# Scanning a state space mixer by rotated states: one scan instruction per block of eight chunks

## The chip, the cores and the metric

The kernel runs on one core of a Trainium2 chip. The metric is device time in microseconds (us) of one execution, given as the median of several runs. The engines are named as the profile names them: PE (TensorE matmul), PEld (its weight loads), DVE (VectorE), ACT (ScalarE), POOL (GpSimd) and SP (SyncE, which issues the DMAs).

## The reference

One inference step of a two-layer decoder trunk over 1,024 prompt tokens and 8 x 4 sample tokens, with a width of 1,024. The change is in one part of layer 0, the state space mixer (S5): 32 groups of 16 channels, each of which drives 64 complex states with a diagonal transition.

```
bu = einsum(u, b_bar)                        # per token: 64 complex inputs per group
s_t = a_bar * s_(t-1) + bu_t                 # complex, elementwise
y_t = Re(c s_t) + D u_t;   out = gelu(y) * sigmoid(gelu(y) @ W + b)
```

Beside it layer 0 has a retention (4 heads) that reads the same normalised input; both outputs go through one projection. Then follow a gated convolutional MLP, layer 1 (a gated linear recurrence with 8 heads) and a second MLP.

## The kernel before, in words

The dense products are made of fp32 numbers split in two parts, three matmuls for each tile of 128 x 128 weights and up to 384 tokens. A job is one weight tile: three token chunks of 24 matmuls each. A planner written by hand puts all other work between these matmuls: a clock `now` counts one unit for a chunk of 24 matmuls, and `at(dt, fn)` emits `fn` when this clock has gone on by `dt`. In layer 0 the order is fixed by these times alone; in layer 1 the planner also looks at its own estimate of what is ready. Each engine runs its instructions in the order in which they were emitted.

The S5 part cuts the 1,024 tokens into 128 chunks of 8. The 32 groups lie along the free dimension, the real parts of the 64 states on partitions 0 to 63 and the imaginary parts on 64 to 127. Its stages:

- `s5_setup` (before the first tile ends) works out the transition and its powers 0 to 8 (`ar`, `ai`) in tiles of 128 x 32; `s5_b` the input matrices; `s5_setup2` the powers 1 to 8 of the transition over one chunk (`mr`, `ms`).
- `s5_x`, 16 pairs of groups: POOL builds a matrix (`va`, `vb`), PE transposes it, ACT copies it (`vt`), PE multiplies it with the chunk's inputs into a PSUM tile `px`. ACT writes the 128 chunk states to `sall`, DVE the sample columns to `xs`. Four calls of `u_work` issue four pairs each.
- `s5_within`, 4 x 7 steps: the 128 chunks are taken as 16 blocks of 8, and step j adds the transition times position j-1 to position j, in all 16 blocks of 8 groups at once. Each step is a complex multiply and add (`s5_mac`: five DVE instructions on 128 columns, two of them on half of the partitions).
- `s5_samples`, one such step for the sample tokens. `s5_carry`, 15 steps in series: the last position of a block gets the last position of the block before, times the transition over a block (five DVE instructions on 32 columns).
- `s5_y`, 16 pairs in 8 calls: `s5_spread` adds the block's incoming state to its other 7 positions (five DVE instructions on 210 columns), POOL, PE and ACT build the output matrices (`ca`, `tz`), and `prod` multiplies `ca` with `sall` and `tz` with the inputs on PE; DVE adds the skip term into `ysh`, and SP stores it.

While these run, PE works on the last tile of the input projection and on those of q, k and v of the retention; DVE and ACT empty their PSUM tiles (`acc`, four buffers, and `misc`, four buffers), and POOL makes part of the weights' low halves (`wlo`) and of the rotary products (`qr`).

Of the kernel before, what the change touches and what calls it, by code (L numbers as in the profile page):

```python
# [10 lines left out]
F32 = mybir.dt.float32  # L11
F32R = mybir.dt.float32r
I32 = mybir.dt.int32
U8 = mybir.dt.uint8
AF = mybir.ActivationFunctionType
OP = mybir.AluOpType
# [30 lines left out]
     "f0": 0.1, "x00": 0.604, "x01": 0.303, "x02": 0.446, "x03": 0.3, "e1": -0.169, "e2": -0.006, "w0": 0.325, "w": 0.274, "sm": 0.432, "ca": 0.308, "ys": 0.020, "r0": 1.195, "rs": 5.046, "h0": 0.1, "hs": 6.5,  # L47
# [183 lines left out]
class Trunk:  # L231
# [414 lines left out]
    def layer0(self):  # L646
# [124 lines left out]
        def u_work(rt):  # L771
            t = P[f"x0{rt}"] + P["x"] * 2 * rt - 3.0 * max(rt - 1, 0)
            x1, x2 = P["x1"] + P["e1"] * (rt == 0), P["x2"] + P["e2"] * (rt == 0)
            for i in range(2):
                self.s5_x(2 * rt + i, t + P["x"] * i, 0.5 * P["x"], x1, x2)
            t += 1.5 * P["x"] + x1 + x2 + P["w0"]
            for j in range(1, 8):
                self.at(t + P["w"] * j, lambda j=j: self.s5_within(8 * rt, 8, j), None,
                        lambda: "powers" not in self.held and self.xdone >= 4 * (rt + 1), "within")
            if rt < 3:  # L780
                return
            t += 7 * P["w"] + P["sm"]
            self.at(t, self.s5_samples, None, lambda: self.xdone == 16)
            for b in range(1, 16):
                self.at(t + P["ca"] * b, lambda b=b: self.s5_carry(b), None,
                        lambda: list(self.wdone.values()) == [7] * 4, "carry")
            for u in range(8):
                self.s5_y(u, t + 15 * P["ca"] + P["ys"] + P["y"] * u, 0.5 * P["y"])
# [137 lines left out]
    def s5_alloc(self):  # L926
        nc, sp = self.nc, self.s5
        self.sall = sp.tile([128, SG, 137], F32, name="sall")
        self.xs = sp.tile([128, SG, NB], F32, name="s_xs")
        nc.gpsimd.memset(self.sall[:, :, 8:9], 0.0)  # L930
# [24 lines left out]
    def s5_load(self):  # L955
        self.nc.sync.dma_start(self.xs, self.I["st_s5"])
        self.bin = []
        for g, n in ((0, 12), (12, 12), (24, 8)):
            t = self.tmp("bin")[:, :2 * n * SH]
            self.nc.sync.dma_start(t.rearrange("p (a c) -> p a c", a=2), self.I["b_in"][:, :, SH * g:SH * (g + n)])  # L960
            self.bin.append(t.rearrange("p (a g h) -> p a g h", a=2, h=SH))
        self.at(0.1, lambda: self.nc.gpsimd.tensor_copy(self.sall[:, :, 0:8], self.xs))

    def s5_setup2(self):

        nc = self.nc
# [27 lines left out]
    def s5_setup(self):  # L994
        nc, sp = self.nc, self.s5
        n = SG

        def small(s):
            return sp.tile([128, n], F32, name=s, tag=s)
        dt, mag, ang, sn, cs = (small(s) for s in ("s_dt", "s_mag", "s_ang", "s_sn", "s_cs"))  # L1000
        lre, lim = self.v("lre"), self.v("lim")
        t = self.tmp("set")
        t = [t[:, n * i:n * i + n] for i in range(9)]
        et, ct = t[:4] + [t[4].bitcast(I32)], t[5:]
# [12 lines left out]
        self.mr = sp.tile([128, SG, 8], F32, name="mr")  # L1017
        self.ms = sp.tile([128, SG, 8], F32, name="ms")
        self.mixed(lambda: self.powers(ar, ai, 1), self.s5_inputs)

    def s5_inputs(self):
# [48 lines left out]
    def s5_x(self, u, t, dt, x1, x2):  # L1070
# [28 lines left out]
        def prod(p, vt):  # L1099
# [9 lines left out]
            nc.scalar.activation(self.sall[:, G, 9:137], pv[:, :, 0:128], AF.Copy)  # L1109
            nc.vector.tensor_copy(self.xs[:, G, :], pv[:, :, 128:136])  # L1110
# [15 lines left out]
    def s5_blocks(self, g, n):  # L1126

        return self.sall[:, g:g + n, 9:137].rearrange("p g (b j) -> p g b j", j=8)

    def s5_samples(self):  # L1130
# [3 lines left out]
        self.s5_mac(self.nc.vector, self.xs, self.sall[:, :, 0:8], self.ar[:, :, 4:5], self.si4[:, :, None], sh, t)  # L1134
        self.put(self.O["s5s"], self.xs)

    def s5_within(self, g, n, j):
        assert "powers" not in self.held and self.xdone >= (g + n) // 2 and self.wdone.get(g, 0) == j - 1
        self.wdone[g] = j
        x = self.s5_blocks(g, n)  # L1140
        sh = [128, n, 16]
        t = [self.tmp("s_t")[:, :16 * n].rearrange("p (g b) -> p g b", b=16) for i in range(2)]
        G = slice(g, g + n)
        self.s5_mac(self.nc.vector, x[:, :, :, j], x[:, :, :, j - 1], self.mr[:, G, 0:1], self.ms[:, G, 0:1], sh, t,
                    self.nc.gpsimd if P["wi"] else None)

    def s5_carry(self, b):
        assert list(self.wdone.values()) == [7] * 4 and self.cdone == b - 1
        self.cdone = b
        x = self.s5_blocks(0, SG)  # L1150
        t = [self.tmp("s_t")[:, :SG] for i in range(2)]
        self.s5_mac(self.nc.vector, x[:, :, b, 7], x[:, :, b - 1, 7], self.mr[:, :, 7], self.ms[:, :, 7], [128, SG], t)
        if b == 15:
            f = self.s5.tile([128, SG], F32, name="s_fin", tag="s_dt")
            self.nc.gpsimd.tensor_copy(f, self.sall[:, :, 136])
            self.put(self.O["s5p"], f)

    def s5_spread(self, g, n, eng):
        assert self.cdone == 15
        x = self.s5_blocks(g, n)  # L1160
        t = [self.tmp("s_t")[:, :105 * n].rearrange("p (g b j) -> p g b j", b=15, j=7) for i in range(2)]
        G = slice(g, g + n)
        sh = [128, n, 15, 7]
        lo, hi = slice(0, 64), slice(64, 128)
        t1, t2 = t
        half = [64] + sh[1:]
        s, d = x[:, :, 0:15, 7:8], x[:, :, 1:16, 0:7]
        mr, ms = self.mr[:, G, None, 0:7], self.ms[:, G, None, 0:7]
        eng.tensor_tensor(t2[hi], s[lo].to_broadcast(half), ms[lo].to_broadcast(half), OP.mult)
        eng.tensor_tensor(t2[lo], s[hi].to_broadcast(half), ms[hi].to_broadcast(half), OP.mult)  # L1170
        eng.tensor_tensor(t1, s.to_broadcast(sh), mr.to_broadcast(sh), OP.mult)
        eng.tensor_tensor(d, d, t2, OP.add)
        eng.tensor_tensor(d, d, t1, OP.add)

    def s5_y(self, u, t, dt):
# [3 lines left out]
        def pair(p):  # L1179
# [4 lines left out]
            self.s5_spread(g, 2, nc.vector if p < P["spV"] else nc.gpsimd)  # L1184
# [23 lines left out]
        def toep(p, bz3, t3, ca3):  # L1208
# [8 lines left out]
            for q in range(4):  # L1217
# [3 lines left out]
                    lambda: [t3, ca3, ld["ut"], self.sall[:, 4 * u + 2 * p:4 * u + 2 * p + 2]],  # L1221
                    lambda: p or self.stored("ysh"), "yprod")

        def prod(p, ca3, t3):
# [5 lines left out]
            for i in range(2):  # L1230
                o = 136 * i
                nc.tensor.matmul(py[:, o:o + 136], ca3[:, i, 32:160], self.sall[:, g + i, 0:136],
                                 start=True, stop=False)
# [1008 lines left out]
```

## Time and profile before

| | |
|---|---|
| median of 3 runs | 2766.38 us (2766.36 to 2770.5) |
| the profiled execution | 2763.77 us, of which the span of its instructions is 2761.6 us |
| mean granted TensorE clock | 0.98 |
| busy: PE, DVE, ACT, POOL | 95%, 58%, 35%, 28% of the span |

Busy shares are means over the whole span. All helpers run through one recorded line (L208), so that instructions are told apart by the tiles that they write and read. "xN" is a count, `out<-in` names the tiles, and a granted clock of 1.00 is TensorE's upper level of 2.4 GHz.

### The profile page before, as it was taken

How to read it: one execution, taken by the hardware profiler on the slowest of the kernel's cores; microseconds unless marked ns; L12 is line 12 of the kernel's file. 1: busy time of each engine (PE TensorE's matmuls, PEld its weight loads, DVE VectorE, ACT ScalarE, POOL GpSimd, SP SyncE). 2: the span in 40 equal slices, each digit the busy share in tenths (PEclk: the TensorE clock that was granted, in tenths of full speed). 3: DMA queues.
4: the chain of work that ended last, by engine and by line, in shares of the span. 5: the costliest groups of instructions: out<-in, count | busy, mean ns of one | idle time of the engine just before them, and what ended most of it. 6: DMA issues, size and time to landing. Idle time of an engine off the chain costs nothing.

```text
span 2761.6 us, 42451 instructions
## 1 busy us (share of the span) xinstructions
PE 2631.6 (95%) x16388; PEld 2593.2 (94%) x16388; DVE 1603.2 (58%) x3261; ACT 971.7 (35%) x2048; POOL 767.3 (28%) x1144
## 2 busy tenths in 40 slices
PE   6778998999999999999999989999999999999998
PEld 5778998999999999999998989989999999999998
DVE  8996664555444444445787887854454444444445
ACT  5223453542212121214444546543422121212225
POOL 4726660421101010102444434431211010101013
PEclk9889999999999999999999999999999999999999
DMA  3412224111111111112211111112111111111112
GB/s 117 96 44 63 66 70 141 42 49 46 47 47 47 47 47 44 49 43 77 86 44 44 52 44 47 48 48 85 65 54 42 50 40 50 43 50 43 46 47 89
DMA packets 110345, 158.70 MB, mean 57 GB/s; under 512 B 18880, under 2 KB 48064, under 8 KB 110144
## 3 DMA queue, kind: packets, MB, share of 16 engines
q1 hardware_dynamic: 109568, 155.41, 18.0%
q8 instruction: 129, 2.11, 0.3%
q14 instruction: 72, 0.59, 0.1%
q10 hardware_dynamic: 576, 0.59, 0.1%
HBM read 135.21 MB, written 20.74 MB: 56 GB/s over the span
## 4 chain that ended last, share of the span: by engine, by line
PE 74%; DVE 17%; ACT 3%; issue 2%; DMA 1%; SPq 1%; POOL 1%; DVEq 0%; ACTq 0%; POOLq 0%
PE acc L208 69%; PE misc L208 5%; DVE s_t L208 2%; DVE hR L208 2%; DVE hF L208 1%; DVE hS L208 1%; DVE rb L208 1%; DVE sall L208 1%; DVE lv L208 1%; SPq L208 1%; DVE nsq L208 1%; DVE hy L208 1%; ACT sTb L208 1%; DMA x<-in_x_dram 0%; DVE hl L208 0%
## 5 line engine op out<-in xcount | busy, mean ns | idle before, releaser
L208 PE MATMUL acc<-hh,whi 128*128 128x384 f32 (+1 forms) x3320 | 1101.9, 332 | 16.2 <-ACT hh L208 6.4
L208 PE MATMUL acc<-hl,whi 128*128 128x384 f32 (+1 forms) x3320 | 1081.9, 326 | 8.1 <-DVE hl L208 8.1
L208 PE MATMUL acc<-hh,wlo 128*128 128x384 f32 (+1 forms) x3320 | 1081.5, 326 | 8.0 <-POOL wlo L208 7.2
L208 PEld LDWEIGHTS acc<-hh,whi 128*128 128x128 f32 x3320 | 630.7, 190 | 20.6 <-ACT whi L208 7.7
L208 PEld LDWEIGHTS acc<-hl,whi 128*128 128x128 f32 x3320 | 630.5, 190 | 12.7 <-DVE hl L208 10.8
L208 PEld LDWEIGHTS acc<-hh,wlo 128*128 128x128 f32 x3320 | 629.7, 190 | 10.9 <-POOL wlo L208 9.5
L208 POOL TENSOR_TENSOR sl<-cv,rstd 128x384 f32<-128x384 f32 (+2 forms) x176 | 151.0, 868 | 1219.8 <-ACT cv L208 1219.8
L208 ACT ACTIVATE whi<-raw 128x512 fp32r<-128x512 f32 x392 | 239.0, 620 | 398.1 <-PE acc L208 386.5
L208 DVE TENSOR_TENSOR x<-acc,x 128x384 f32<-128x384 f32 (+1 forms) x360 | 187.6, 523 | 281.1 <-PE acc L208 280.8
L208 DVE TENSOR_TENSOR wlo<-raw,whi 128x512 fp32r<-128x512 f32 x298 | 238.7, 801 | 140.7 <-ACT whi L208 137.8
L208 PE MATMUL acc<-hdl,whi 128*128 128x384 f32 (+1 forms) x984 | 317.9, 323 | 0.0
L208 PE MATMUL acc<-hdh,wlo 128*128 128x384 f32 (+1 forms) x984 | 317.7, 323 | 0.0
L208 PE MATMUL acc<-hdh,whi 128*128 128x384 f32 (+1 forms) x984 | 317.4, 323 | 0.0
L208 DVE SCALAR_TENSOR_TENSOR cv<-ext,vec,cv 128x384 f32<-128x384 f32 (+1 forms) x264 | 156.0, 591 | 173.1 <-ACT cv L208 168.4
L208 PE MATMUL acc<-ys,whi 128*128 128x384 f32 (+1 forms) x768 | 189.7, 333 | 12.5 <-DVE x L208 4.8
L208 ACT ACTIVATE cv<-ext,vec 128x384 f32<-128x384 f32 x132 | 90.7, 687 | 287.9 <-DVE ext L208 226.7
L208 PEld LDWEIGHTS acc<-hdl,whi 128*128 128x128 f32 x984 | 184.9, 188 | 0.3
L208 PEld LDWEIGHTS acc<-hdh,whi 128*128 128x128 f32 x984 | 184.8, 188 | 0.3
L208 PEld LDWEIGHTS acc<-hdh,wlo 128*128 128x128 f32 x984 | 185.0, 188 | 0.0
L208 POOL TENSOR_TENSOR wlo<-raw,whi 128x512 fp32r<-128x512 f32 x98 | 134.0, 1370 | 171.9 <-ACT whi L208 151.0
L208 ACT ACTIVATE hdh<-sl 128x384 fp32r<-128x384 f32 x132 | 65.9, 499 | 249.3 <-DVE sl L208 249.3
L208 PEld LDWEIGHTS acc<-ys,whi 128*128 128x128 f32 x768 | 138.0, 193 | 15.8 <-DVE x L208 5.1
(316 smaller groups left out, 3362.0 us busy)
## 6 DMA issues: line engine op xcount, KB each, us to landing
raw<-in_w_gate_dram SPq DMA_DIRECT2D x88, 256.0 KB, 2.6
raw<-in_w_up_dram SPq DMA_DIRECT2D x88, 256.0 KB, 2.6
raw<-in_w_dn_dram SPq DMA_DIRECT2D x88, 256.0 KB, 2.6
raw<-in_w_c_dram SPq DMA_DIRECT2D x64, 256.0 KB, 2.7
raw<-in_w_ab_dram SPq DMA_DIRECT2D x40, 256.0 KB, 2.8
x<-in_x_dram SPq DMA_DIRECT2D x15, 528.0 KB, 7.8
ush<-uD SPq DMA_DIRECT2D x128, 34.0 KB, 1.9
xD<-x SPq DMA_DIRECT2D x8, 528.0 KB, 2.9
```

Source lines behind the costliest of these rows:

```text
L208: return fn(*a, **k)
```

## The change

The states of a block are held in a rotated frame. With the transition over a chunk written as a magnitude `m8` and an angle, position j of a block is multiplied by the angle's conjugate j times. In that frame the recurrence within a block is real, and DVE's scan instruction does it: one instruction for all 32 groups and 8 positions of one block, with a zero factor at position 0 of each group.

- `sall` is laid out by block (17 x 32 x 8) in place of by group (32 x 137).
- `s5_turn` is new: 15 small DVE instructions in `s5_setup` that square the angle's sine and cosine three times and the magnitude with them. `s5_setup2` then makes powers of the rotation alone, loses two copies and gains two products, one copy and a memset on POOL (`mz`, the factors of the scan). `s5_inputs` loses one small instruction.
- In `prod` of `s5_x`, ACT writes the sample columns, position 0 of each block and the last state in three small copies; DVE rotates the other 7 positions straight from PSUM (`s5_rotate`: four instructions on 224 columns, two of them on half of the partitions), in place of its copy of the sample columns.
- `s5_within` and `s5_carry` go. `s5_block`, 16 steps in series, is a scan on 256 columns and one `s5_mac` on 32 columns that carries the end of the block to position 0 of the next. The planner's spacing of these steps goes from 0.308 to 0.42 units; the 7 x 0.274 units of `s5_within` go.
- In `s5_y`, `s5_rotate` turns the block back (four instructions on 224 columns) in place of `s5_spread`, and the matmul with `ca` reads `sall` as 17 runs of 8 columns.

```diff
-     "w": 0.274, "sm": 0.432, "ca": 0.308, "ys": 0.020,
+     "w": 0.274, "sm": 0.432, "ca": 0.42, "ys": 0.020,
...
-            for j in range(1, 8):
-                self.at(t + P["w"] * j, lambda j=j: self.s5_within(8 * rt, 8, j), ...)
...
-            t += 7 * P["w"] + P["sm"]
+            t += P["sm"]
             self.at(t, self.s5_samples, None, lambda: self.xdone == 16)
-            for b in range(1, 16):
-                self.at(t + P["ca"] * b, lambda b=b: self.s5_carry(b), ...)
+            for b in range(1, 17):
+                self.at(t + P["ca"] * b, lambda b=b: self.s5_block(b), None, lambda: self.xdone == 16, "carry")
...
-                self.s5_y(u, t + 15 * P["ca"] + P["ys"] + P["y"] * u, 0.5 * P["y"])
+                self.s5_y(u, t + 16 * P["ca"] + P["ys"] + P["y"] * u, 0.5 * P["y"])
...
-        self.sall = sp.tile([128, SG, 137], F32, name="sall")
+        self.sall = sp.tile([128, 17, SG, 8], F32, name="sall")
...
+    def s5_turn(self, mag, sn, cs, t):
...
+        a, b, c = t
+        for i in range(3):
+            r, q = (cs, sn) if i == 0 else (b, c)
+            nr, nq = (self.mr[:, :, 0], self.ms[:, :, 0]) if i == 2 else (b, c)
+            nc.vector.tensor_tensor(a, q, q, OP.mult)
+            nc.vector.scalar_tensor_tensor(nq, r, 2.0, q, OP.mult, OP.mult)
+            nc.vector.tensor_tensor(nr, r, r, OP.mult)
+            nc.vector.tensor_tensor(nr, nr, a, OP.subtract)
+            nc.vector.tensor_tensor(self.m8, mag if i == 0 else self.m8, mag if i == 0 else self.m8, OP.mult)
...
-            nc.scalar.activation(self.sall[:, G, 9:137], pv[:, :, 0:128], AF.Copy)
-            nc.vector.tensor_copy(self.xs[:, G, :], pv[:, :, 128:136])
+            nc.scalar.activation(self.xs[:, G, :], pv[:, :, 128:136], AF.Copy)
+            nc.scalar.activation(self.sall[:, 2:17, G, 0].rearrange("p b g -> p g b"), pv[:, :, 7:127:8], AF.Copy)
+            nc.scalar.activation(self.xfin[:, G], pv[:, :, 127], AF.Copy)
+            self.s5_rotate(G, pv[:, :, 0:128].rearrange("p g (b j) -> p g b j", j=8)[:, :, :, 0:7], OP.subtract)
...
+    def s5_rotate(self, G, src, op):
...
+        nc.vector.tensor_tensor(t2[hi], src[lo], ms[lo].to_broadcast([64] + sh[1:]), OP.mult)
+        nc.vector.tensor_tensor(t2[lo], src[hi], ms[hi].to_broadcast([64] + sh[1:]), OP.mult)
+        nc.vector.tensor_tensor(t1, src, mr.to_broadcast(sh), OP.mult)
+        nc.vector.tensor_tensor(d, t1, t2, op)
...
+    def s5_block(self, b):
...
+        x = self.sall[:, b].rearrange("p g j -> p (g j)")
+        nc.vector.tensor_tensor_scan(x, self.mz.rearrange("p g j -> p (g j)"), x, 0.0, OP.mult, OP.add)
+        t = [self.tmp("s_t")[:, :SG] for i in range(2)]
+        d = self.xfin if b == 16 else self.sall[:, b + 1, :, 0]
+        self.s5_mac(nc.vector, d, self.sall[:, b, :, 7], self.kr, self.ks, [128, SG], t)
...
-            self.s5_spread(g, 2, nc.vector if p < P["spV"] else nc.gpsimd)
+            self.s5_rotate(slice(g, g + 2), None, OP.add)
...
-                nc.tensor.matmul(py[:, o:o + 136], ca3[:, i, 32:160], self.sall[:, g + i, 0:136],
+                nc.tensor.matmul(py[:, o:o + 136].rearrange("p (b j) -> p b j", j=8), ca3[:, i, 32:160],
+                                 self.sall[:, :, g + i], start=True, stop=False)
```

## Rows read from the trace of the kernel before

**Rows 1.** Windows: stretch, length, busy us of each engine (instructions), granted clock, DMA.

```profile
85.00:163.70 78.70, 63.77 (x376) 61.28 (x377) 73.33 (x167) 22.36 (x54) 46.82 (x84) 0.90 0.29 72
163.70:215.00 51.30, 38.90 (x227) 37.99 (x226) 48.51 (x142) 12.32 (x28) 13.77 (x15) 0.87 0.11 35
215.00:420.00 205.00, 197.75 (x1355) 194.28 (x1355) 123.66 (x257) 96.65 (x237) 130.80 (x206) 0.97 0.25 67
```

**Rows 2.** Waits of PE from 85 to 215 us: total us, times, longest.

```profile
PE misc L208 <- DVE S L208: 12.4, 3, 7.1
...
PE misc L208 <- POOL va L208: 4.7, 3, 2.0
PE misc L208 <- POOL ush L208: 2.9, 2, 2.5
```

**Rows 3.** Windows of DVE instructions with the S5 temporaries `s_t` alone.

```profile
85.00:163.70 78.70, 52.16 (x105) 0.90 0.29 72
163.70:215.00 51.30, 39.11 (x115) 0.87 0.11 35
```

**Rows 4.** DVE groups by shape, 85 to 163.7 us: busy us, mean ns.

```profile
L208 DVE COPY s_xs<-misc 128x16 f32<-128x16 f32 x16 | 2.6, 165 | 0.0
```

**Rows 5.** PE in order of time at the end of the first tiles; its idle time in brackets.

```profile
63.78 0.61 PE L208 MATMUL acc<-hh,whr 128*128 128x288 f32 x1 [5.43 <-ACT us L208]
...
74.48 0.69 PE L208 MATMUL misc<-ident,va 128*128 128x128 f32 x2 [9.61 <-POOL va L208]
```

**Rows 6.** DVE instructions of the setup's tile, 36 to 50 us: ns min/median/max.

```profile
L208 DVE SCALAR_TENSOR_TENSOR set<-set x8: 179/180/183, 35.9 to 40.8; 128x32 f32<-128x32 f32 x8
```

**Rows 7.** DVE groups by shape, 163.7 to 215 us.

```profile
L208 DVE TENSOR_TENSOR s_t<-sall,ms 64x32 f32<-64x32 f32 x30 | 9.4, 312 | 0.7
...
L208 DVE TENSOR_TENSOR sall<-sall,s_t 128x32 f32<-128x32 f32 x30 | 6.5, 216 | 0.5
L208 DVE TENSOR_TENSOR s_t<-sall,mr 128x32 f32<-128x32 f32 x15 | 6.2, 417 | 0.5
...
L208 DVE SCALAR_TENSOR_TENSOR S<-S,misc 128x128 f32<-128x128 f32 x5 | 1.4, 284 | 0.1
...
L208 DVE TENSOR_TENSOR s_t<-sall,s_si 64x256 f32<-64x256 f32 x2 | 1.5, 768 | 0.0
...
L208 DVE TENSOR_TENSOR s_xs<-s_xs,s_t 128x256 f32<-128x256 f32 x2 | 0.8, 422 | 0.0
L208 DVE TENSOR_TENSOR s_t<-sall,ar 128x256 f32<-128x256 f32 x1 | 0.4, 426 | 0.0
```

**Rows 8.** DVE groups by shape, 215 to 420 us.

```profile
L208 DVE TENSOR_TENSOR s_t<-sall,ms 64x210 f32<-64x210 f32 x32 | 20.0, 624 | 5.2 <-POOL bc L208 3.3 <-PE misc L208 0.9 <-POOL qr L208 0.4
L208 DVE TENSOR_TENSOR sall<-sall,s_t 128x210 f32<-128x210 f32 x32 | 16.9, 529 | 0.6
...
L208 DVE TENSOR_TENSOR s_t<-sall,mr 128x210 f32<-128x210 f32 x16 | 9.4, 586 | 0.6
...
L208 DVE TENSOR_TENSOR qr<-acc,ct 128x288 f32<-128x288 f32 x4 | 1.8, 458 | 3.2 <-ACT rt L208 3.2
```

**Rows 9.** DVE's scans in layer 1, whole span: ns min/median/max.

```profile
L208 DVE TENSOR_TENSOR_SCAN hS<-f,endA x16: 925/932/1987, 1357.4 to 1787.2; 128x384 f32<-128x384 f32 x16
L208 DVE TENSOR_TENSOR_SCAN hS<-f,endB x8: 726/1116/1802, 1381.9 to 1806.1; 128x288 f32<-128x288 f32 x8
```

**Rows 10.** DVE in order of time: the first instructions of two carries in a row.

```profile
205.26 0.43 DVE L208 TENSOR_TENSOR s_t<-sall,ms 64x32 f32<-64x32 f32 x2
...
206.38 0.45 DVE L208 TENSOR_TENSOR s_t<-sall,ms 64x32 f32<-64x32 f32 x2
```

**Rows 11.** PE in order of time: one product with `sall` and what follows it.

```profile
231.56 0.39 PE L208 MATMUL misc<-sall,ca 128*128 128x136 f32 x2
231.79 0.40 PE L208 MATMUL misc<-ush,tz 128*128 128x136 f32 x2
```

**Rows 12.** Waits of PE from 215 to 420 us.

```profile
PE misc L208 <- DVE ysh L208: 5.8, 3, 3.2
```

More of the change, by code (lines that the diff above doesn't have):

```diff
@@ L1002, in s5_setup @@
         t = self.tmp("set")
-        t = [t[:, n * i:n * i + n] for i in range(9)]
-        et, ct = t[:4] + [t[4].bitcast(I32)], t[5:]
+        t = [t[:, n * i:n * i + n] for i in range(12)]
+        et, ct = t[:4] + [t[4].bitcast(I32)], t[5:9]
         self.exp(dt, self.v("ldt"), n, et)
@@ L1016, in s5_setup @@
         self.s5t = mag, sn, cs
-        self.mr = sp.tile([128, SG, 8], F32, name="mr")
-        self.ms = sp.tile([128, SG, 8], F32, name="ms")
+        self.s5_turn(mag, sn, cs, t[9:])
         self.mixed(lambda: self.powers(ar, ai, 1), self.s5_inputs)
@@ L1124, in s5_mac @@
         eng.tensor_tensor(d, d, t1, OP.add)
-    def s5_blocks(self, g, n):
-        return self.sall[:, g:g + n, 9:137].rearrange("p g (b j) -> p g b j", j=8)
+    def s5_rotate(self, G, src, op):
+        nc = self.nc
+        n = G.stop - G.start
+        d = self.sall[:, 1:17, G, 1:8].rearrange("p b g j -> p g b j")
+        src = d if src is None else src
+        t1, t2 = (self.tmp("s_t")[:, :112 * n].rearrange("p (g b j) -> p g b j", b=16, j=7) for i in range(2))
+        lo, hi = slice(0, 64), slice(64, 128)
+        sh = [128, n, 16, 7]
+        mr, ms = self.mr[:, G, None, 0:7], self.ms[:, G, None, 0:7]
+        nc.vector.tensor_tensor(t2[hi], src[lo], ms[lo].to_broadcast([64] + sh[1:]), OP.mult)
+        nc.vector.tensor_tensor(t2[lo], src[hi], ms[hi].to_broadcast([64] + sh[1:]), OP.mult)
+        nc.vector.tensor_tensor(t1, src, mr.to_broadcast(sh), OP.mult)
+        nc.vector.tensor_tensor(d, t1, t2, op)
     def s5_samples(self):
@@ L1133, in s5_samples @@
         t = [self.tmp("s_t")[:, :SG * NB].rearrange("p (g b) -> p g b", b=NB) for i in range(2)]
-        self.s5_mac(self.nc.vector, self.xs, self.sall[:, :, 0:8], self.ar[:, :, 4:5], self.si4[:, :, None], sh, t)
+        self.s5_mac(self.nc.vector, self.xs, self.sall[:, 0], self.ar[:, :, 4:5], self.si4[:, :, None], sh, t)
         self.put(self.O["s5s"], self.xs)
[L1137 to L1145, printed above, removed]
@@ L1147, in s5_carry @@
-    def s5_carry(self, b):
-        assert list(self.wdone.values()) == [7] * 4 and self.cdone == b - 1
+    def s5_block(self, b):
+        assert self.xdone == SG // 2 and self.cdone == b - 1 and "powers" not in self.held
         self.cdone = b
-        x = self.s5_blocks(0, SG)
+        nc = self.nc
+        x = self.sall[:, b].rearrange("p g j -> p (g j)")
+        nc.vector.tensor_tensor_scan(x, self.mz.rearrange("p g j -> p (g j)"), x, 0.0, OP.mult, OP.add)
         t = [self.tmp("s_t")[:, :SG] for i in range(2)]
[L1152 to L1173, printed above, removed]
+        d = self.xfin if b == 16 else self.sall[:, b + 1, :, 0]
@@ L1175, in s5_y @@
+        self.s5_mac(nc.vector, d, self.sall[:, b, :, 7], self.kr, self.ks, [128, SG], t)
+        if b == 16:
+            self.put(self.O["s5p"], self.xfin)
     def s5_y(self, u, t, dt):
@@ L1247, in s5_y @@
             self.at(t + p * dt, lambda p=p: pair(p), None,
-                    lambda: "bc" in ld and self.cdone == 15 and ("zb", p) not in self.held, "ypair")
+                    lambda: "bc" in ld and self.cdone == 16 and ("zb", p) not in self.held, "ypair")
     def rot_load(self):
```

34 lines of the change are left out of this document (19 added, 15 removed).

## Prediction

> **What bounds the kernel now.** I read the page first: PE is busy nearly all the time, so a change off PE counts only where PE stands still. The page's forty slices put those places at the start, around the boundaries of the layers and in layer 1; S5 lies in the first. The timeline of DVE then gave the limits of its stages, and the windows over them are [rows 1]. I call 85 to 163.7 us stage X (inputs to states, with 21 of the 28 steps of `s5_within`), 163.7 to 215 us stage B (the last seven steps, the samples, the 15 carries) and 215 to 420 us stage Y.
>
> The reader is to see that DVE is full in X and B, 73.3 of 78.7 us and 48.5 of 51.3 us, while PE issues 376 and 227 matmuls there at granted clocks of 0.90 and 0.87. In Y it is the other way round: PE 197.8 of 205 us with 1,355 matmuls, DVE at 60% [rows 1]. At Y's pace, 1355 / 205 = 6.61 matmuls per us, the matmuls of X would take 56.9 us and those of B 34.3 us. So PE loses up to 21.8 us in X and 17 us in B. Who holds it: the waits of PE name DVE's `S`, a state of the retention that stands in DVE's queue behind S5, with 12.4 us, against 4.7 and 2.9 us for POOL's `va` and `ush` [rows 2]. Of DVE's time the instructions with `s_t`, nearly all of them S5, take 52.2 us in X and 39.1 us in B [rows 3]. DVE is the bound of 130 us of the kernel, and S5 is 75% of its load there; after that PE is.
>
> **Part 1, the setup: a loss.** PE waits 5.4 us for ACT's `us` and 9.6 us for POOL's `va` at the end of the first tiles [rows 5]. Both stand behind DVE's setup: `s5_b` needs its result, ACT takes `s5_b`'s output before it can do the norm's statistics, and POOL's `va` needs both. `s5_turn` puts 15 instructions of 32 columns into that line, one `s5_inputs` instruction leaves. A setup instruction of this size takes 0.180 us [rows 6]: (15 - 1) x 0.18 = 2.5 us, with nothing to hide it. With the 0.312 us that a 32-column instruction on half the partitions took amid POOL's work [rows 7] it would be 4.4 us. In `s5_setup2` two copies go and three small instructions come; I set that to zero, since the steps that need it follow later.
>
> **Part 2, stage X.** Removed from DVE: 52.2 us of `s5_within` [rows 3] and 16 copies of the sample columns, 2.6 us [rows 4]. Left of it is 73.3 - 52.2 - 2.6 = 18.5 us. Added: 16 x 4 instructions on 224 columns. No row has them. Three of the four read PSUM and one SBUF tensor; with such operands 128 columns took 0.284 us [rows 7] and 288 took 0.458 us [rows 8], so 224 lie near 0.39 us. The fourth reads two SBUF tensors and writes runs of 7, as `s5_spread` does: 0.529 us [rows 8]. That is 16 x (3 x 0.39 + 0.53) = 27.2 us. At the prices of `s5_spread` throughout, 16 x (2 x 0.624 + 0.586 + 0.529) = 37.8 us [rows 8]. DVE then has 45.7 us (56.3 at most) of work for PE's 56.9 us, and PE is the bound. I don't expect it to reach 56.9: its waits for `va` and `ush`, 7.6 us [rows 2], come from POOL and a transfer that the change leaves alone. I take 56.9 + 7.6 = 64.5 us, a gain of 14.2 us; 56.9 us (a gain of 21.8) is one bound, and the other, with DVE at 56.3 us and the waits it then still causes, I set at 70 us (8.7).
>
> The prices rest on what a second SBUF operand does next to POOL. The rows: `qr`, with one operand in PSUM, took 0.458 us for 288 columns, while `s_t` and `sall`, with both in SBUF, took 0.53 to 0.62 us for 210 [rows 8], next to a POOL that is busy 64% of that stage [rows 1]. The Trainium skill (SBUF — State Buffer, "Who interferes with whom") says why: a VectorE instruction with two SBUF inputs and a GpSimd instruction that reads SBUF lock each other out, one with a single SBUF input doesn't. The traces agree so far, and by that rule the three PSUM reads pay nothing for POOL: 27.2 us and not 37.8.
>
> ACT gets three small copies for one of 256 columns, 32 more in all, and is busy 22 of 78.7 us [rows 1]: nothing. The `misc` tile of `px` is released by DVE in both kernels, now three instructions later, about 1.2 us, out of four buffers: nothing as long as DVE isn't behind.
>
> **Part 3, stage B.** Left of DVE's work is 48.5 - 39.1 = 9.4 us and the samples, 1.5 + 0.8 + 0.4 = 2.7 us [rows 7], together 12.1 us. Added are 16 blocks. The complex step on 32 columns is the old carry: (9.4 + 6.5 + 6.2) / 15 = 1.47 us [rows 7], and 1.12 us from one to the next where nothing disturbs it [rows 10]. The scan: at best 0.925 us for 384 columns and 0.726 us for 288 [rows 9], 2.07 ns a column, so 0.66 us for 256; at worst the 1.12 us that is the median for 288. POOL is light here, 13.8 of 51.3 us [rows 1], so I take 0.70 us. A block is 2.17 us (1.78 to 2.59), all 16 are 34.7 us (28.5 to 41.4), and DVE has 46.8 us (40.6 to 53.5). At the share that it has now, 48.5 of 51.3, the stage takes 49.5 us (43 to 56.6): a gain of 1.8 us, between a gain of 8.3 and a loss of 5.3. DVE stays the bound here: PE's 34.3 us grow by 7.172 - 6.988 = 0.18 units, under 1 us. What is late behind a block on DVE is still `S` and the evacuations of `qr`, for which PE waits.
>
> **Part 4, stage Y.** DVE drops from five instructions to four for each pair, 46.3 us [rows 8] to about 38 us. PE bounds this stage and hides DVE, so I take zero; at most the 5.8 us that PE waits for `ysh` [rows 12] could shrink, and I allow 3. The matmuls with `sall` read runs of 8 columns, 1 KB apart. No row has such an operand; the nearest is the contiguous one, 0.23 us [rows 11], and I take the same. The flush before the last tile of the retention comes at the same unit as before, and the transfers after it are the same. In layer 1 the planner's estimates start from other times, and its order may change a little; I allow 2 us either way.
>
> **Sum.** +2.5 - 14.2 - 1.8 + 0 = -13.5 us. The profiled execution took 2763.8 us (span 2761.6), so it would be 2750.3 us; the median of the runs lies 2.6 us higher, and from it the forecast is 2766.4 - 13.5 = 2752.9 us. A difference of 0.2%, 5.5 us, is about what a measurement of this kernel can tell from no change.
>
> **Rivals.** First, both stages come down to their floors: X to 56.9 us, B to 43 us, `ysh` helps by 3. For it: an idle PE also loses clock here, 0.90 and 0.87 against 0.97 in Y [rows 1], and gets it back with fewer gaps. Against it: POOL's waits remain. 2.5 - 21.8 - 8.3 - 3 = -30.6: 2736 us.
>
> Second, X is held by POOL, and the change moves the queue from DVE to it. For it: POOL is busy 46.8 of 78.7 us in X [rows 1], and `va` and `ush` already stop PE there [rows 2]. Against it: POOL's 46.8 us hold locks that fewer two-operand DVE instructions would release. If X gives back only 5 us and B nothing, 2.5 - 5 = -2.5: 2764 us, no change that can be told.
>
> Third, on the other side: the matmuls with `sall` pay for their broken-up operand. There are 32 products of 0.23 us [rows 11], all in the stage that PE bounds, so whatever they lose is lost in full. Twice the price costs 7.4 us and leaves a gain of 6; from 3.6 times (0.83 us each) on, the kernel is slower by over 0.2%; at four times it loses 22.1 us, 2766.4 - 13.5 + 22.1 = 2775 us. Nothing in the trace speaks for it or against it. The Trainium skill (SBUF — State Buffer, on "cachelines") says that accesses which fall into the same 16 bytes run at full rate and that each new line costs; runs of 8 fp32 fill two lines, so by it the price is nil.
>
> **How the numbers follow.** The forecast, with sums from -8 to -21 us (2745 to 2758 us), gets 0.50; the floors 0.20; POOL 0.20; the matmuls, or the blocks at their worst price together with a held X, 0.10. The range goes from the first rival's 2736 to the point where the unknown prices are all bad but X still gains a little: 2737 to 2766 us leaves out half of the slow cases above and a tail below, 2 in 10. Faster by over 0.2%: the forecast, the floors and a few of the second rival's, 0.73; within 0.2%: most of the second, 0.18; slower: 0.09.
>
> **What would show it.** Right: in X the share of DVE falls to about 70% and the stage ends some 14 us earlier relative to its start; PE's waits for `S` fall; the rotations from PSUM take 0.38 to 0.46 us and no more next to POOL; a scan on 256 columns 0.66 to 0.75 us; blocks follow each other at 2.0 to 2.4 us with DVE still full; PE's gap before the first transpose grows by 2.5 us. Wrong: X as long as before with POOL full, scans above 1 us, or products with `sall` above 0.23 us.

## The result, and the profile after

| | before | after |
|---|---|---|
| median of the runs | 2766.37 us (2763.62 to 2770.5, 4 runs) | 2744.63 us (2742.69 to 2748.95, 4 runs) |
| ratio of the two, 95% interval | | 0.9922 (0.9905 to 0.994) |
| the profiled execution, its span | 2763.77 us, 2761.6 us | 2748.95 us, 2747.2 us |

The kernel is faster by 21.7 us, with an interval of 17 to 26 us; the forecast was 13.5 us. The profiled execution of after is the longest of its four runs, so the traces explain only 14.4 us of span.

The windows of after are cut at the first product with `ush`, the end of the last rotation, the first rotation back, the last product with `sall` and the first `hdh` matmul, which opens the MLP of layer 0. X and B of [rows 1] end within half a us of matching events: before has no rotation, so its X ends when DVE has taken the sample columns of the last pair, and its B still holds the last seven steps of `s5_within`. The columns are stretch, length, busy us of PE, PEld, DVE, ACT and POOL (instructions), granted clock, DMA share, GB/s:

```profile
87.00:151.30 64.30, 60.44 (x374) 59.39 (x375) 49.01 (x113) 21.44 (x86) 45.79 (x84) 0.92 0.36 88
151.30:203.20 51.90, 40.92 (x247) 39.69 (x245) 48.55 (x131) 13.32 (x30) 18.35 (x22) 0.87 0.11 35
203.20:396.60 193.40, 187.35 (x1301) 183.62 (x1302) 119.48 (x233) 93.68 (x233) 126.00 (x196) 0.98 0.26 71
396.60:611.90 215.30, 206.48 (x1235) 203.24 (x1234) 112.62 (x193) 98.05 (x169) 52.81 (x69) 0.97 0.24 77
```

Y of before up to its last product, and its boundary from there to the first `hdh`:

```profile
215.10:413.10 198.00, 190.75 (x1314) 187.28 (x1313) 119.06 (x247) 94.01 (x234) 128.74 (x203) 0.97 0.26 69
413.10:630.30 217.20, 207.04 (x1239) 203.72 (x1238) 113.89 (x196) 99.22 (x171) 52.56 (x69) 0.97 0.24 76
```

Against before: up to the start of X +2.0 us (85.0 to 87.0), X -14.4 (78.7 to 64.3), B +0.5 (51.4 to 51.9), Y up to its last product -4.6 (198.0 to 193.4), the boundary from there to the first `hdh` matmul -1.9 (217.2 to 215.3), the rest +4.0 (2131.3 to 2135.3). The sum is -14.4 us.

The reader is to see that X has turned over: DVE is busy 49.0 of 64.3 us, where it was 73.3 of 78.7 [rows 1], and PE 60.4. B has not: DVE still has 48.6 of 51.9 us, and PE's clock there is still 0.87.

The waits of PE, first in X, then in B: us in total, times, longest. The wait for the transfer of `ush` ends with the first product at 86.86 us, so it lies before X; in X itself PE stands idle for 3.9 us. In B DVE's `S` is still the one that holds it, 11.0 us against the 12.4 of [rows 2]:

```profile
PE misc L208 <- DVE s_t L208: 2.9, 1, 2.9
PE misc L208 <- DMA ush<-uD: 2.9, 1, 2.9
PE misc L208 <- POOL ush L208: 0.8, 1, 0.8
...
PE misc L208 <- DVE S L208: 11.0, 3, 5.7
```

The new instructions by their tiles over the whole span (ns min/median/max, first and last start): the rotations from PSUM, the scan, and the products with `sall`.

```profile
L208 DVE TENSOR_TENSOR s_t<-misc,ms x32: 383/389/395, 91.3 to 150.2; 64x224 f32<-64x224 f32 x32
L208 DVE TENSOR_TENSOR s_t<-misc,mr x16: 390/392/393, 92.1 to 150.6; 128x224 f32<-128x224 f32 x16
...
L208 DVE TENSOR_TENSOR_SCAN sall<-mz,sall x16: 682/684/1423, 155.0 to 201.5; 128x256 f32<-128x256 f32 x16
...
L208 PE MATMUL misc<-sall,ca x64: 277/279/434, 217.5 to 396.6; 128*128 128x136 f32 x64
```

The products with `sall` before the change:

```profile
L208 PE MATMUL misc<-sall,ca x64: 277/279/431, 231.6 to 413.1; 128*128 128x136 f32 x64
```

Of 48 rotations from PSUM the slowest takes 395 ns, though POOL is busy 71% of that stage. The scan has a median of 684 ns, but some take twice that. The products' median is the 279 ns that it was before the change, when their operand was contiguous.

The blocks in B, groups of DVE by shape (busy us, mean ns):

```profile
L208 DVE TENSOR_TENSOR_SCAN sall<-mz,sall 128x256 f32<-128x256 f32 x16 | 13.1, 820 | 0.1
L208 DVE TENSOR_TENSOR s_t<-sall,s_ks 64x32 f32<-64x32 f32 x32 | 11.8, 369 | 1.0
L208 DVE TENSOR_TENSOR sall<-sall,s_t 128x32 f32<-128x32 f32 x30 | 6.5, 216 | 0.5
L208 DVE TENSOR_TENSOR s_t<-sall,s_kr 128x32 f32<-128x32 f32 x16 | 5.4, 335 | 0.5
```

Two blocks in order of time (start us, us), the first held up at its pair of 64x32 products, the second undisturbed:

```profile
178.80 0.68 DVE L208 TENSOR_TENSOR_SCAN sall<-mz,sall 128x256 f32<-128x256 f32 x1
179.52 2.07 DVE L208 TENSOR_TENSOR s_t<-sall,s_ks 64x32 f32<-64x32 f32 x2
...
182.11 0.60 DVE L208 SCALAR_TENSOR_TENSOR S<-S,misc 128x128 f32<-128x128 f32 x2
182.63 0.68 DVE L208 TENSOR_TENSOR_SCAN sall<-mz,sall 128x256 f32<-128x256 f32 x1
183.34 0.43 DVE L208 TENSOR_TENSOR s_t<-sall,s_ks 64x32 f32<-64x32 f32 x2
...
184.30 0.41 DVE L208 TENSOR_TENSOR yr<-misc,qdec 128x256 f32<-128x256 f32 x1
```

The second block is done in 184.30 - 182.63 = 1.67 us, the first in 182.11 - 178.80 = 3.31 us, of which 1.6 us lie in one pair of small products that otherwise takes 0.43 us. POOL ran two instructions just then, and the pair ended when the second of them did:

```profile
179.03 1.26 POOL L208 TENSOR_TENSOR qr<-qr,rt 128x384 f32<-128x384 f32 x1 [2.91 <-DVE rt L208]
180.26 1.27 POOL L208 TENSOR_TENSOR wlo<-raw,whi 128x512 fp32r<-128x512 f32 x1
```

At the end of the first tiles PE's gap in front of the first transpose is as long as in [rows 5], but it ends 1.5 us later. The gap that has grown is the one before it, PE's wait for ACT's `us`, 7.55 us for 5.43:

```profile
65.27 0.61 PE L208 MATMUL acc<-hh,whr 128*128 128x288 f32 x1 [7.55 <-ACT us L208]
75.97 0.69 PE L208 MATMUL misc<-ident,va 128*128 128x128 f32 x2 [9.61 <-POOL va L208]
```

### The profile page after: what moved, and what is told of

It is laid out like the page before. It is cut to its first block, busy times and chain, and to the rows that moved or that the text cites. A ratio compares the mean times of both kernels' runs of the same rounds, so it can differ in the third digit from the quotient of the medians.

```text
span 2747.2 us, 42440 instructions
## 1 busy us (share of the span) xinstructions
PE 2632.8 (96%) x16388; PEld 2593.6 (94%) x16388; DVE 1579.2 (57%) x3189; ACT 970.1 (35%) x2080; POOL 769.8 (28%) x1144
## 4 chain that ended last, share of the span: by engine, by line
PE 77%; DVE 14%; ACT 3%; issue 2%; POOL 1%; SPq 1%; DMA 1%; DVEq 0%; POOLq 0%; ACTq 0%
PE acc L208 71%; PE misc L208 6%; DVE hR L208 1%; DVE hF L208 1%; DVE rb L208 1%; DVE hS L208 1%; DVE lv L208 1%; DVE nsq L208 1%; SPq L208 1%; DVE set L208 1%; DVE s_t L208 1%; DVE hy L208 1%; ACT sTb L208 0%; DVE hl L208 0%; DVE sacc L208 0%
## 5 line engine op out<-in xcount | busy, mean ns | idle before, releaser
L208 PE MATMUL acc<-hh,whi 128*128 128x384 f32 (+1 forms) x3320 | 1102.0, 332 | 18.0 <-ACT whi L208 8.1
L208 PE MATMUL acc<-hh,wlo 128*128 128x384 f32 (+1 forms) x3320 | 1081.5, 326 | 9.2 <-POOL wlo L208 8.4
L208 PE MATMUL acc<-hl,whi 128*128 128x384 f32 (+1 forms) x3320 | 1081.6, 326 | 8.0 <-DVE hl L208 7.9
L208 PEld LDWEIGHTS acc<-hh,whi 128*128 128x128 f32 x3320 | 630.6, 190 | 22.5 <-ACT whi L208 10.4
L208 PEld LDWEIGHTS acc<-hl,whi 128*128 128x128 f32 x3320 | 630.3, 190 | 13.2 <-DVE hl L208 11.6
L208 PEld LDWEIGHTS acc<-hh,wlo 128*128 128x128 f32 x3320 | 629.4, 190 | 12.5 <-POOL wlo L208 11.1
L208 POOL TENSOR_TENSOR sl<-cv,rstd 128x384 f32<-128x384 f32 (+2 forms) x176 | 151.1, 869 | 1219.4 <-ACT cv L208 1219.4
L208 ACT ACTIVATE whi<-raw 128x512 fp32r<-128x512 f32 x392 | 239.0, 620 | 397.9 <-PE acc L208 386.6
L208 DVE TENSOR_TENSOR x<-acc,x 128x384 f32<-128x384 f32 (+1 forms) x360 | 187.4, 522 | 281.2 <-PE acc L208 280.9
L208 DVE TENSOR_TENSOR wlo<-raw,whi 128x512 fp32r<-128x512 f32 x298 | 238.6, 801 | 140.1 <-ACT whi L208 137.3
L208 PE MATMUL acc<-hdl,whi 128*128 128x384 f32 (+1 forms) x984 | 317.9, 323 | 0.0
L208 PE MATMUL acc<-hdh,wlo 128*128 128x384 f32 (+1 forms) x984 | 317.7, 323 | 0.0
L208 PE MATMUL acc<-hdh,whi 128*128 128x384 f32 (+1 forms) x984 | 317.3, 323 | 0.0
L208 DVE SCALAR_TENSOR_TENSOR cv<-ext,vec,cv 128x384 f32<-128x384 f32 (+1 forms) x264 | 155.9, 590 | 173.8 <-ACT cv L208 169.2
L208 PE MATMUL acc<-ys,whi 128*128 128x384 f32 (+1 forms) x768 | 189.5, 332 | 10.8 <-DVE x L208 4.2
L208 ACT ACTIVATE cv<-ext,vec 128x384 f32<-128x384 f32 x132 | 90.7, 687 | 288.9 <-DVE ext L208 227.6
L208 PEld LDWEIGHTS acc<-hdh,whi 128*128 128x128 f32 x984 | 184.8, 188 | 0.3
L208 PEld LDWEIGHTS acc<-hdl,whi 128*128 128x128 f32 x984 | 184.8, 188 | 0.3
L208 PEld LDWEIGHTS acc<-hdh,wlo 128*128 128x128 f32 x984 | 185.0, 188 | 0.0
L208 POOL TENSOR_TENSOR wlo<-raw,whi 128x512 fp32r<-128x512 f32 x98 | 134.2, 1372 | 162.7 <-ACT whi L208 145.6
L208 ACT ACTIVATE hdh<-sl 128x384 fp32r<-128x384 f32 x132 | 65.9, 499 | 248.5 <-DVE sl L208 248.5
L208 PEld LDWEIGHTS acc<-ys,whi 128*128 128x128 f32 x768 | 138.3, 194 | 13.9 <-DVE x L208 4.5
```

Source lines behind the costliest of these rows:

```text
L208: return fn(*a, **k)
```

## The experiments

Each experiment changes the kernel after; its ratio is to the kernel before on the same chip, and rules divide the chips. The last column is the place of the first `hdh` matmul in the profile. It reads layer 0 alone; from there to the end every kernel takes 2125 to 2136 us, 2131.3 before.

| run | median, us | ratio (95% interval) | first `hdh`, us |
|---|---|---|---|
| before / after | 2766.37 / 2744.63 | 0.9922 (0.9905 to 0.994) | 630.3 / 611.9 |
| ------ | | | |
| X rotated twice | 2759.61 | 0.998 (0.9968 to 0.9991) | 625.1 |
| late turn | 2742.97 | 0.9915 (0.9897 to 0.9932) | 604.2 |
| no carry | 2727.44 | 0.9863 (0.9845 to 0.9881) | 591.3 |
| order of before | 2744.41 | 0.9922 (0.9905 to 0.9938) | 606.8 |
| ------ | | | |
| rotation from SBUF | 2751.34 | 0.9956 (0.9942 to 0.9969) | 614.9 |
| blocks closer | 2735.5 | 0.9901 (0.9888 to 0.9915) | 602.4 |
| blocks wider | 2739.58 | 0.9913 (0.99 to 0.9925) | 601.8 |
| Y with five | 2739.1 | 0.9914 (0.99 to 0.9928) | 610.6 |
| ------ | | | |
| combined | 2725.15 | 0.9858 (0.9841 to 0.9875) | 594.0 |
| early end | 2732.17 | 0.9883 (0.9868 to 0.9898) | 599.4 |
| after again | 2741.86 | 0.9913 (0.99 to 0.9927) | 609.9 |

**X rotated twice.** Does DVE's load set the length of X? All rotations of X are done twice:

```diff
-        nc.vector.tensor_tensor(t2[hi], src[lo], ...)   # and the three that follow
+        for i in range(2 if op == OP.subtract else 1):
+            nc.vector.tensor_tensor(t2[hi], src[lo], ...)   # and the three that follow
```

> The changed kernel with every rotation of the states in stage X done twice: 64 more DVE instructions, about 16 x 1.56 = 25 us of DVE work put back. If DVE's load set stage X before (my theory), DVE has 49 + 25 = 74 us in a stage that now lasts 64 us, the stage goes back to about 76 us and the kernel to 2756 us. If the gain came from the new order and fewer temporaries, with DVE merely busy, DVE's 15 idle us take most of it and the kernel loses 0 to 4 us.

X by its window:

```profile
87.00:166.50 79.50, 63.54 (x390) 60.29 (x389) 74.67 (x174) 22.22 (x88) 46.00 (x85) 0.96 0.29 69
```

With 74.7 us of DVE work X is 79.5 us long, as it was before with 73.3 in 78.7 [rows 1], and the gain is all but gone. DVE's load in X is what the change took away, and what set that stage. Of PE's waits 7.4 us are named for POOL, which had 0.8 us in after, though POOL's own work is the same:

```profile
PE misc L208 <- POOL ush L208: 4.1, 3, 1.8
PE misc L208 <- POOL va L208: 3.3, 3, 1.4
```

**Late turn, order of before.** The second keeps after as it is but starts the planner of layer 1 with the clock that it had in the kernel before, so that layer 1 keeps its order (`shift` moves all of the planner's estimated times); the first does that too, and moves the turn behind `s5_b`, into time that DVE stood idle, with tiles of their own for what `s5_inputs` would overwrite (line L208 is L221 there):

```diff
+            self.ahead.shift(1300226.557333 - self.ahead.at["tensor"], {...})      # both
...
-        self.s5_turn(mag, sn, cs, t[9:])                                       # late turn
-        den, nr, t = mag, sn, cs
+        den, nr, t = small("s_den", "s_dt"), small("s_nr", "s_si4"), small("s_tt", "s_ang")
...
         self.s5_b()
+        self.s5_turn(*self.s5t, [self.tmp("turn")[:, :SG] for i in range(3)])
```

> The changed kernel with the 15 setup instructions moved behind the input matrices, where DVE stands idle for 6 us and waits for ACT; layer 1 in the order that the kernel before has. If the setup lies on the path that ends in PE's first transpose, that transpose comes 1.5 us earlier than in the changed kernel (76.0 us) and the kernel is 1.5 us below the run that changes layer 1's order alone. If it is hidden: no difference between the two.

> The changed kernel with layer 1 emitted in the order that it has in the kernel before (the planner's own clock is set to the same time at the start of layer 1; nothing else differs). In the profiles the changed kernel is 18.4 us ahead at the first MLP but only 14.4 us at the end. If the new order of layer 1 costs these 4 us, this kernel takes 2740 us or less. If they are variation between executions, it takes the changed kernel's 2744.6 us within 2 us.

With the late turn the first transpose starts at 73.5 us (75.8 in the order of before, 76.0 in after, 74.5 before), the wait for `us` is 5.43 us again, and the first `hdh` stands 2.6 us before that of the order of before:

```profile
62.86 0.61 PE L221 MATMUL acc<-hh,whr 128*128 128x288 f32 x1 [5.43 <-ACT us L221]
73.55 0.69 PE L221 MATMUL misc<-ident,va 128*128 128x128 f32 x2 [9.60 <-POOL va L221]
```

So the turn's cost reaches PE, 2.1 us in that wait, as said; by the times the two aren't told apart. The order of layer 1 makes no difference by the times (0.9922 both). In the profiles the rest from the first `hdh` on is 2128.8 us with the old order and 2135.3 in after; but the late turn and, below, the combined kernel, with the old order too, show 2131.8 and 2136.3. My thought that the new order costs 4 us is not borne out.

**No carry.** What is B worth without the carry? Fifteen of the 16 blocks leave out their complex step, so the blocks no longer hang together:

```diff
+        if b == 16:
             self.s5_mac(nc.vector, d, self.sall[:, b, :, 7], self.kr, self.ks, [128, SG], t)
```

> The changed kernel without the complex step that carries the end of a block to the next (left out for 15 of 16 blocks; the scans stay): 75 DVE instructions less, about 18 us. If stage B is still bound by DVE, it falls from 52 us to PE's pace, 247 matmuls at 6.61 per us = 37 us and some waits, about 40 us, and the kernel to 2733 us. If PE, POOL or transfers hold stage B, it stays at 50 us or more.

B by its window:

```profile
147.70:187.30 39.60, 39.60 (x266) 38.92 (x265) 32.81 (x55) 13.31 (x30) 21.59 (x27) 1.00 0.14 46
```

With 15.7 us less on DVE, B is 12.3 us shorter, PE has no gap, no wait for `S`, and clock 1.00. B of after is still DVE's, and the carry is its price.

**Rotation from SBUF.** Do the rotations owe their price to PSUM? ACT first copies `px`, and the rotations read two SBUF tensors:

```diff
-            self.s5_rotate(G, pv[...], OP.subtract)
+            nc.scalar.activation(sx, px[:, :272], AF.Copy)
+            self.s5_rotate(G, sv[...], OP.subtract)
```

> The changed kernel with an ACT copy of the chunk states to SBUF ahead of the rotations of stage X, which then read two SBUF tensors each in place of PSUM and SBUF. If two SBUF operands make DVE wait for POOL, the 48 instructions that took 0.39 us from PSUM take 0.6 to 0.7 us on average as they do in stage Y, DVE gets some 12 us more in stage X, has little idle time left there, and the stage goes from 64 to 66 or 70 us: the kernel loses 2 to 6 us. If the operand's place costs nothing they stay at 0.39 us and the kernel at 2744 us.

```profile
L208 DVE TENSOR_TENSOR s_t<-sx,ms x32: 384/493/1383, 90.1 to 155.3; 64x224 f32<-64x224 f32 x32
L208 DVE TENSOR_TENSOR s_t<-sx,mr x16: 391/492/1395, 90.9 to 155.7; 128x224 f32<-128x224 f32 x16
```

The shortest are the same, 384 and 391 ns; the median rises from 389 to 493 and the longest from 395 to 1,395. Those that meet no POOL instruction in time take 0.39 us as before, and every longer one overlaps one. So the operand's place costs nothing in itself, only next to POOL. X, from the first product with `ush` to the end of the last rotation, takes 70.3 us instead of 64.3, and the ratio loses 0.0034 to 0.0043, 9 to 12 us, more than I expected. But DVE is busy for 57.4 of the 70.3 us, not full, and PE's waits are POOL's, which pays too: its `va` products take 548 ns in the median in X for 404 in after.

```profile
PE misc L208 <- POOL va L208: 5.7, 3, 2.5
PE misc L208 <- POOL ush L208: 3.1, 3, 1.6
```

What of the loss comes from the collisions and what from ACT's copy, which now stands ahead of the rotations, was not separated.

**Blocks closer, blocks wider, Y with five.** The spacing of the blocks is 0.308 units as the old carries had it, or 0.55 (there with the outputs closer, so that the last comes at about the same unit); the third gives Y its fifth DVE instruction per pair back:

```diff
-    "ca": 0.42                 "y": 3.5
+    "ca": 0.308                              # blocks closer
+    "ca": 0.55                 "y": 3.22     # blocks wider
...
-        nc.vector.tensor_tensor(t1, src, mr.to_broadcast(sh), OP.mult)
+        for i in range(2 if op == OP.add else 1):      # Y with five
+            nc.vector.tensor_tensor(t1, src, mr.to_broadcast(sh), OP.mult)
```

> The changed kernel with the blocks spaced 0.308 units apart, as the carries were before, in place of 0.42: 1.8 units, 43 matmuls or 6.5 us of PE work, move from stage B to stage Y. If DVE bounds stage B, the stage stays at 50 us with less PE work under it, and the kernel loses about 6 us: 2751 us. If the spacing was what held stage B, it gets shorter and the kernel stays or gains.

> The changed kernel with the blocks spaced 0.55 units apart and the calls of the output stage 3.22 units apart in place of 0.42 and 3.5, so that the outputs end at the same unit: 2.1 units, 50 matmuls or 7.5 us of PE work, move under stage B. If DVE bounds stage B and PE bounds stage Y, the kernel gains 4 to 7 us: 2739 us. If stage Y can't hold its work in 26 units in place of 28, what stage B gains is lost there and the kernel stays at 2744 us.

> The changed kernel with one of the four rotation instructions of stage Y done twice, so that each pair of groups costs DVE five instructions as it did before. From the first outputs to the last product with the states the kernel before took 198 us and the changed one 193.4 us in the profiles. If DVE's fifth instruction is behind these 4.6 us, the stretch goes back to 197 or 198 us and the kernel loses 4 us. If it is the start from a better place, or variation, the stretch stays at 192 to 194 us.

Stages B and Y with the blocks wider:

```profile
149.00:204.20 55.20, 52.30 (x341) 51.16 (x340) 52.86 (x139) 15.64 (x36) 21.34 (x24) 0.97 0.14 43
204.20:387.00 182.80, 174.54 (x1205) 170.76 (x1204) 110.70 (x221) 90.91 (x227) 122.36 (x192) 0.97 0.28 72
```

B takes 3.3 us more than in after and issues 94 matmuls more; PE waits 2.9 us for `S`, not 11.0, and the clock is 0.97. Y has that much less to do. The first `hdh` comes 8 to 10 us earlier, though the time does not follow (0.9913, as after again).

The closer blocks were a miss. I had expected a loss, since B then offers PE still fewer matmuls; B did have only 195 of them in 45.8 us, but the first `hdh` came 7.5 to 9.5 us earlier. The closer blocks also end the outputs 16 x 0.112 = 1.8 units earlier, which I had not counted. By the time alone (2735.5 us) it isn't told apart from after, the intervals overlap.

With five instructions Y takes 196.0 us, between the two answers:

```profile
200.60:396.60 196.00, 188.00 (x1303) 184.04 (x1304) 124.44 (x249) 93.95 (x234) 127.33 (x195) 0.98 0.27 70
```

The six profiles with four instructions and the same spacing of blocks and outputs (after twice, late turn, order of before, rotation from SBUF, X rotated twice) have 191.2 to 193.4 us, and PE is idle for 5.4 to 6.1 us in them against 8.0 us here. So the instruction costs Y 2.6 to 4.8 us as far as one profile can tell. The time shows no loss (0.9914), and the first `hdh` stands at 610.6 us, where after has it (609.9 and 611.9), but X is 61.6 us long in this profile, 1.0 to 2.7 us shorter than in those two.

**Early end, after again, combined.** The first leaves the blocks alone and ends the outputs 1.8 units earlier; the second is the kernel after, unaltered; the third joins the late turn, the wide blocks and the early end:

```diff
-    "ca": 0.42     "y": 3.5
+                   "y": 3.26     # early end
+    "ca": 0.55     "y": 2.98     # combined, with the late turn and the order of before
```

> The changed kernel with the outputs' spacing 3.26 instead of 3.5, the blocks left as they are, so that the last output is due about 1.8 units earlier, as in the run with the blocks' spacing 0.308. Theory (that run gained because its outputs ended earlier): the stretch of the blocks stays at 51 to 53 us, the first MLP starts 5 to 9 us earlier than in the changed kernel, about 2738 us. Rival (it gained by the blocks themselves being put closer together): no change, 2743 to 2746 us, and the closer blocks are the cause.

> The changed kernel once more, unaltered, beside the two others on the same chip, so that they are compared with it directly. Expected: 0.992 of the kernel before, about 2744 us; the place of its first MLP (611.9 us in the first profile) moves by no more than 3 us if the profiles of two executions can be compared at that level, and by more if the differences of 4 to 8 us between profiled stretches are execution noise.

> The late turn, the wider spacing of the blocks (0.55) and outputs that end about 1.9 us earlier (0.24 off their spacing) together, with layer 1 in the order of the kernel before. Theory (the three gains lie in three stretches and add up: 2.3 us at the first transpose, 5 to 7 us in the stretch of the blocks by fewer waits for DVE, about 5 us behind the last product): first MLP of layer 0 after about 596 us, and about 2732 us for the whole against about 2744 for the changed kernel. Rival (what the blocks gain is only work that is then missing as cover behind the outputs, as the Y stretch shortened by 10 us when the blocks' stretch took more filler): not below 2738 us, no more than the wide blocks alone.

The early end is 9.7 us faster than after again on the same chip, 2731.2 to 2735.5 against 2736.7 to 2745.5, and its blocks are those of after (B 51.1 us). The outputs' earlier end by itself is therefore enough for the miss above. After again puts the first `hdh` 2.0 us from the first profile's place, within the 3 us expected. What stands behind the early end, first in after: PE's waits behind the last product, then SP's queue in order of time.

```profile
PE acc L208 <- DVE x L208: 4.2, 1, 4.2
PE acc L208 <- ACT ys L208: 3.4, 2, 3.2
PE acc L208 <- DVE ys L208: 1.1, 2, 0.6
```

```profile
400.12 4.47 SPq L208 DMA_DIRECT2D yD<-ysh  x8
...
405.61 4.99 SPq L208 DMA_DIRECT2D x<-in_x_dram  x8
411.53 13.11 SPq L208 DMA_DIRECT2D yl<-yD  x8
```

The same of the early end:

```profile
PE acc L208 <- DVE x L208: 1.9, 1, 1.9
PE acc L208 <- DVE ys L208: 1.8, 2, 1.0
PE acc L208 <- ACT ys L208: 0.2, 1, 0.2
```

```profile
385.34 3.64 SPq L208 DMA_DIRECT2D yD<-ysh  x8
...
390.00 11.59 SPq L208 DMA_DIRECT2D x<-in_x_dram  x8
401.64 11.32 SPq L208 DMA_DIRECT2D yl<-yD  x8
```

The last outputs go to DRAM (`yD`) and come back as `yl`, behind the loads of `x`; the projection's `ys` needs them. That chain starts 14.8 us earlier, with more matmuls left to cover it, and PE waits 3.9 us for `x` and `ys` instead of 8.7. From the end of B to 600 us the early end issues 2,543 matmuls in 398 us; after again issues 2,534 up to 610 us in 408.5. Idle PE falls from 15.2 to 9.1 us there, and the other 4 us go with a higher clock, 1.00 for 0.98 in Y and 0.98 for 0.97 behind it.

Combined, B:

```profile
148.20:203.40 55.20, 52.30 (x341) 51.17 (x340) 52.89 (x139) 15.55 (x36) 21.35 (x24) 0.97 0.13 39
```

The first `hdh` comes 16 to 18 us before that of after, and the median is 2725.15 us, 16.7 us below after again and 1.4% below the kernel before. It is the lowest median of all the runs. More than half of the 16.7 us is the early end's 9.7: the combined kernel lies 7.0 us below that run, and their intervals overlap a little. The theory's 2732 us was reached by the early end alone, so 2725 us does not refute the rival that the wide blocks only borrow cover from Y; whether the wide blocks add anything to the early end is not shown.

## Why the prediction was right, and where its sizes were off

**X: the mechanism right, its size in part by luck.** X was forecast at 64.5 us and is 64.3 in the first profile. The rotations from PSUM were put at 0.39 us and take 0.389 and 0.392; the four together come to 28.2 us against 27.2, since the fourth takes 0.60 us and not 0.53. DVE has 49.0 us, not 45.7, which costs nothing below PE's 60.4. The double rotation shows that it was DVE's load that went.

The second term of X failed: the 7.6 us of waits for `va` and `ush`, taken as POOL's own, which the change would leave alone. In X PE is idle for 3.9 us, and 0.8 us of it is named for POOL, so the second rival, X held by POOL, is out. The trace of before could have shown that DVE stood behind part of these waits. The waits for `S` that were set against them [rows 2] all lie in B; in X PE waited 6.2 us for DVE's `vf`, and POOL itself stood 11.8 us for DVE:

```profile
PE misc L208 <- DVE vf L208: 6.2, 2, 4.2
POOL qr L208 <- DVE rt L208: 6.0, 2, 3.9
POOL qr L208 <- DVE s_xs L208: 5.8, 2, 3.8
```

In after POOL stands 2.7 us for DVE in X, and with the rotations doubled 17.0 us, with 7.4 us of PE's waits named for POOL again. The sum came out all the same because the matmuls kept PE busy for 60.4 us, where 56.9 us at Y's pace was to hold them with their gaps. After's second profile and the order of before, with the same X, are shorter at a higher clock:

```profile
86.80:149.40 62.60, 59.25 (x375) 58.33 (x376) 48.77 (x114) 21.32 (x86) 45.93 (x85) 0.95 0.38 91
86.80:148.40 61.60, 57.93 (x375) 56.80 (x376) 47.61 (x114) 21.32 (x86) 46.42 (x84) 0.97 0.39 93
```

So hitting X to 0.2 us was luck: two misses that cancel, in a profile whose granted clock there is 0.92.

**The port: right.** The Trainium skill's rule (SBUF — State Buffer, "Who interferes with whom") had been used for the rotations' price. The rotation from SBUF agrees with it: the same instruction has the same minimum from either place, its median rises by 104 ns with two SBUF operands, and the longer ones are those that meet a working POOL.

**Setup: right in sign, smaller in size.** The first transpose starts 1.5 us later, against +2.5. The turn itself was about right: its 15 instructions take 2.25 us on DVE and lengthen PE's wait for `us` by 2.1 us, in both profiles of after, and the late turn takes all of that away. What is left of the difference is that PE reaches this wait earlier than before the change, 65.27 - 7.55 = 57.72 us for 63.78 - 5.43 = 58.35 us [rows 5]; why was not followed. The sign that the prediction gave, a longer gap in front of the transpose itself, did not show: that gap stayed at 9.61 us.

**B: mis-sized.** Forecast -1.8 us, measured +0.5. The blocks take 13.1 + 11.8 + 6.5 + 5.4 = 36.8 us, 2.30 us each, not 34.7. The scan is the term: 0.684 us by the median, as the 0.70 said, but 0.820 us in the mean, since some of them, like some of the small products, meet a POOL that I had called light: all eight instructions and pairs of the blocks that take over 0.9 us overlap one of POOL's. That DVE stays the bound of B, and that `S` is what PE waits for, was right, as the run without the carry and the wide blocks show.

**Y: taken as zero, measured -4.6 us, with -1.9 at the boundary.** This is the step that made the forecast too small. The third rival is out: the products take 279 ns as before. The rule on cachelines (the Trainium skill, SBUF — State Buffer) had it so. In Y PE issues 13 matmuls fewer (1,301 for 1,314; B has 19 more of the common stock), about 2 us at 6.6 per us; the waits for `ysh`, 5.8 us [rows 12], are gone, with others in their place, 1.2 us less in all; the rest, about 1.5 us, goes with PE's clock, 0.98 for 0.97. The prediction's reason for zero, that PE hides DVE in Y, does not hold in full: with the fifth instruction put back Y is 2.6 to 4.8 us longer and PE idle for 2 us more. That is one profile, and the times do not show it. The waits for `ysh` did not come back with it; why they went was not tried.

**The sum.** Layer 0 up to the first `hdh` gained 18.4 us, and 20.4 in the second profile, where the terms said 13.5. In the first profile Y and the boundary gave 6.5 us more than said, the setup 0.5 and X 0.2, and B 2.3 us less; in the second X gave 1.9 us more as well. In layer 1 the 2 us either way were too few: single profiles range over 11 us (2125 to 2136) whatever the change. The profile's 14.4 us look like the forecast because 4 us of that noise stand against it, which is luck. By the runs the forecast is 8 us too high: the measured 21.7 us lie just beyond the 8 to 21 us that it had named, within the range, and 9 us short of the first rival's floors.

## What to carry to other kernels

Cut the span at events of the algorithm and set each engine's work in a stage against the matmuls that the stage has: a load taken off DVE is worth the stage's surplus over PE's floor and no more, and a stage where the surplus remains (B here) gives nothing. In a schedule written out by hand the new lengths leave the old spacing wrong, and ending the outputs earlier was worth another 9.7 us, or 16.7 us together with the blocks at a wider spacing and the turn out of the way. Look at the last event of a stage by what transfers start behind it, not only by the stage's own length.

## What the runs showed of the hardware

- A two-operand DVE instruction of 224 columns takes 383 to 395 ns when one operand is in PSUM, in all 48 cases beside a POOL that is busy 71% of the time; with both in SBUF it took 384 to 1,395 ns, and POOL's `va` products beside it took 548 ns in the median for 404.
- Small instructions lose most beside their own time: a pair of 32-column products of 0.43 us took 2.07 us while POOL ran two instructions of 1.26 and 1.27 us. A chain of them in series is priced by the mean, not by the undisturbed row.
- A matmul whose moving operand lies in 17 runs of 8 columns, 1 KB apart, took 279 ns in the median, as with the contiguous one.
- PE's granted clock in B, a mean over stretches at its two levels, was 0.87 where PE waited 11 us for `S` (after), 0.97 where it waited 2.9 us (wide blocks), and 1.00, the 2.4 GHz level throughout, where it did not wait (no carry). The sum of the waits alone does not tell it: in X it was 0.92 with 3.9 us of idle PE (after) and 0.96 with 16.0 us (X rotated twice).
